# One plain float32 k-tile instead of two, six k-tiles of the first modulation summed on TensorE, idle matmuls and silu(c) at the head of a transformer block

## The chip, the cores and the metric

The kernel runs on one core of a Trainium2 chip. The metric is the device time of one execution in microseconds (us), lower is better; the median of several runs is compared.

## The reference, cut to what matters

One block of depth 1, with batch 1, T = 256 tokens, D = 2048 and float32 throughout. A vector c gives six rows of modulation (shift, scale and gate, for the mixer and for the feed-forward part), and x goes through a mixer and a feed-forward net:

```python
mod = jax.nn.silu(c) @ w_ada[l] + b_ada[l]                 # c: 1 x 2048, w_ada: 2048 x 12288
shift_m, scale_m, gate_m, shift_f, scale_f, gate_f = jnp.split(mod, 6, axis=-1)
h = modulate(rms_norm(x, pre_norm_mix[l]), shift_m, scale_m)   # h * (1 + scale) + shift
... = jnp.split(h @ w_in[l], split_at, axis=-1)             # w_in: 2048 x 5656
o = jnp.concatenate([nsa_mixer(...), moba_mixer(...)], axis=-1) @ w_o[l]
x = x + gate_m[:, None, :] * rms_norm(o, post_norm_mix[l])
h = modulate(rms_norm(x, pre_norm_ffn[l]), shift_f, scale_f)
f = jnp.square(jax.nn.relu(h @ w_up[l])) @ w_down[l]        # 2048 x 8192 and back
x = x + gate_f[:, None, :] * rms_norm(f, post_norm_ffn[l])
```

All weights together are some 300 MB, and each is read once.

## The kernel before, in words

**Products.** A k-tile is 128 of the 2048 columns of h. Nearly every product is made of three: activation and weight are each split into a high and a low part of type fp32r (`split`, L544 on ScalarE and L545 on VectorE for a weight, `split2`, L417 and L418 for an activation), and `products` (L549 to L551) multiplies high by high, high by low and low by high into one PSUM bank. Where k is under `M_PLAIN` (two k-tiles before), `weight_units` takes one plain float32 matmul instead (L497) and splits nothing; the trace shows such a matmul as two records.

**Modulation.** The rows shift and scale are needed as columns, one value a partition. `mod_units` makes them for 2 or 4 k-tiles at a time (`M_MODS`): `gemv_units` loads the matching columns of w_ada for all 2048 rows (L305), VectorE accumulates weight times silu(c) over 16 k-tiles of rows (L318 and L323), and TensorE adds the 128 partitions up. For the first group (tile `modm0`), the k-tiles in `M_DIRECT` (3, 7, 11) go to TensorE at once, as matmuls with a single column (`column_sums`, L359), and the accumulated rest follows with a column of ones. The bias enters by a matmul with the identity (L356). The other groups are transposed (L377) and reduced on VectorE (L379). Then ScalarE (L414) and, for the second k-tile, VectorE (L400) modulate `xnm`, the normalised and transposed x.

**The head.** `x_units` loads x in four pieces (L573), squares it on ScalarE (L579), scales it on VectorE (L584) and transposes it on TensorE (L283; L285 copies back). c is loaded first, b_ada and the two norms next (L205 to L208, ScalarE's queue); silu(c) is L189 to L214, `columns` L216 to L223.

**Order.** `Stream.run` walks a list of units. A unit has a load, a preparation (a split, or VectorE's accumulation) and a main part (products). At most `RAWBUFS` = 5 loaded tiles may be held: a tile is given back after its preparation, or for plain products after its main part. All loads go through SyncE's queue in list order. The list starts with x, the group `modm0`, then the blocks of w_in (kv, kw, qn, vm, km, qm, each 1024 columns wide, kw 536) for k = 0 and 1, with the eight loads and the end of the next group (`modm2`, k = 2 to 5) strewn between them by `spread` (L1000). Then come the blocks for k = 2 to 5 with the next group between them, and so on. The order of instructions on each engine is fixed when the program is built, from list order, priority (`high_priority`) and readiness; each engine then works in that order. `late_constants` (L244) loads the rope table and small weights amid this, and transposes `stageb` (L257).

**The end.** The last unit multiplies token-major. After a bank's last product, `down_done` squares it on ScalarE (L1229) and multiplies by the gate on VectorE (L1230); `finish` sums four squares (L269), makes the reciprocal root (L273, L274 on GpSimd) and writes x (L1238, L1241).

## Time and profile before

| | |
|---|---|
| three runs | 1189.11, 1190.44, 1192.91 us; median 1190.44 us |
| profiled execution | 1188.98 us, of which the span from first to last instruction is 1187.2 us |
| busy in the span | TensorE 1154.3 us, VectorE 901.4 us, ScalarE 592.8 us |
| DMA | 312.03 MB, mean 263 GB/s |

In the profile PE is TensorE (PEld its weight loads), DVE VectorE, ACT ScalarE, POOL GpSimd and SP SyncE; a q behind a name is the engine's queue, where DMAs are issued. Times in rows are us from the start of the span unless marked ns. TensorE is busy nearly throughout, so that what matters is where it waits, and what it does while it only seems busy.

### The profile page before, as it was taken

Reading aid. Unit: us, or ns where it says so; the run is one execution under the profiler, and the core shown is the slowest. Engines: PE = TensorE matmul, PEld = TensorE weight load, DVE = VectorE, ACT = ScalarE, POOL = GpSimd, SP = SyncE. Lnnn points to the kernel's source line nnn. Section 1 sums busy time; section 2 is a strip of 40 time slices with the busy share of each in tenths; the row PEclk is TensorE's granted clock in tenths of the full one; section 3 lists DMA queues with packets and bytes.
Section 4 is the critical chain, followed back from the end, with each engine's and each line's share of the span. In section 5 each row is a group of like instructions: output and inputs, shape, how many; then the busy total and the mean of one; then the engine's idle time right before and its main releaser. Section 6 shows DMA issues by size and latency. Waiting matters only on the chain.

```text
span 1187.2 us, 14413 instructions
## 1 busy us (share of the span) xinstructions
PE 1154.3 (97%) x5411; PEld 935.7 (79%) x5411; DVE 901.4 (76%) x1111; ACT 592.8 (50%) x908; POOL 13.5 (1%) x23
## 2 busy tenths in 40 slices
PE   5999999999999998999999999999999999999997
PEld 4468888877777786888888888888888888888885
DVE  5679999889999988777888986666576666665573
ACT  4353444438746658565343344767444434444441
POOL 1000000000000001000000000000000000000000
PEclk9999999999999999999999999999999999999999
DMA  9999998775867985988878976545677777775541
GB/s 333 370 394 326 334 362 295 238 281 176 316 213 258 327 337 200 367 285 305 290 249 300 315 248 204 172 152 208 238 244 270 255 258 264 259 268 187 203 142 71
DMA packets 92601, 312.03 MB, mean 263 GB/s; under 512 B 6306, under 2 KB 14962, under 8 KB 79602
## 3 DMA queue, kind: packets, MB, share of 16 engines
q1 hardware_dynamic: 92324, 311.04, 74.7%
q8 instruction: 42, 0.69, 0.2%
q14 instruction: 27, 0.22, 0.1%
q10 hardware_dynamic: 208, 0.07, 0.0%
HBM read 308.99 MB, written 2.10 MB: 262 GB/s over the span
## 4 chain that ended last, share of the span: by engine, by line
PE 88%; DVE 7%; ACT 1%; issue 1%; DMA 1%; POOL 0%; SPq 0%; DVEq 0%; POOLq 0%; ACTq 0%
PE dps L550 10%; PE dps L551 10%; PE dps L549 10%; PE up L551 9%; PE up L550 9%; PE up L549 9%; PE wo L550 2%; PE wo L549 1%; PE wo L551 1%; PE ft L1146 1%; PE in_qm L551 1%; PE in_qm L549 1%; PE in_qm L550 1%; PE in_km L549 1%; PE in_km L550 1%
## 5 line engine op out<-in xcount | busy, mean ns | idle before, releaser
L323 DVE SCALAR_TENSOR_TENSOR modm<-modm,csil,modm 128x1024 f32<-128x1024 f32 (+1 forms) x72 | 78.3, 1087 | 9.4 <-DMA modm<-in_w_ada_dram 8.0
L323 DVE SCALAR_TENSOR_TENSOR modf<-modf,csil,modf 128x1024 f32<-128x1024 f32 x60 | 76.8, 1280 | 5.6 <-DMA modf<-in_w_ada_dram 5.2
L1162 DVE TENSOR_TENSOR facc<-up,facc 128x512 f32<-128x512 f32 x96 | 61.5, 685 | 19.2 <-PE up L551 19.2
L323 DVE SCALAR_TENSOR_TENSOR gatef<-gatef,csil,gatef 128x1024 f32<-128x1024 f32 x32 | 40.6, 1280 | 1.7 <-DMA gatef<-in_w_ada_dram 1.7
L323 DVE SCALAR_TENSOR_TENSOR gatem<-gatem,csil,gatem 128x1024 f32<-128x1024 f32 x32 | 40.3, 1275 | 0.0
L1202 DVE TENSOR_TENSOR flo<-facc,fhi 128x512 fp32r<-128x512 f32 x32 | 21.8, 686 | 2.0 <-ACT fhi L1201 2.0
L1201 ACT CAST fhi<-facc 128x512 fp32r<-128x512 f32 x32 | 19.7, 624 | 5.3 <-PE up L550 1.9
L1164 ACT ACTIVATE facc<-facc 128x512 f32<-128x512 f32 x32 | 18.4, 623 | 2.8 <-DVE facc L1162 2.8
L1160 ACT COPY facc<-up 128x512 f32<-128x512 f32 x32 | 18.0, 586 | 1.7 <-PE up L551 1.0
L545 DVE TENSOR_TENSOR up_13lo<-up,up_13hi 128x1024 fp32r<-128x1024 f32 x8 | 9.8, 1226 | 11.5 <-ACT up_13hi L544 11.5
L545 DVE TENSOR_TENSOR up_14lo<-up,up_14hi 128x1024 fp32r<-128x1024 f32 x8 | 9.8, 1226 | 11.1 <-ACT up_14hi L544 11.1
L1151 ACT ACTIVATE facc<-ft 128x512 f32<-128x512 f32 x32 | 17.1, 586 | 0.4 <-PE ft L1146 0.2
L1146 PE MATMUL ft<-ident,facc 128*128 128x128 f32 x128 | 16.8, 273 | 0.0
L1146 PEld LDWEIGHTS ft<-ident,facc 128*128 128x128 f32 x128 | 14.7, 140 | 2.6 <-ACT facc L1151 0.4
L544 ACT CAST up_7hi<-up 128x1024 fp32r<-128x1024 f32 x8 | 8.4, 1056 | 14.2 <-PE up L551 14.2
L544 ACT CAST up_11hi<-up 128x1024 fp32r<-128x1024 f32 x8 | 8.4, 1056 | 14.2 <-PE up L551 14.2
L544 ACT CAST up_10hi<-up 128x1024 fp32r<-128x1024 f32 x8 | 8.4, 1056 | 13.3 <-PE up L551 13.3
L544 ACT CAST up_6hi<-up 128x1024 fp32r<-128x1024 f32 x8 | 8.4, 1056 | 13.3 <-PE up L551 13.3
L544 ACT CAST up_14hi<-up 128x1024 fp32r<-128x1024 f32 x8 | 8.4, 1049 | 12.6 <-PE up L551 12.6
L544 ACT CAST up_9hi<-up 128x1024 fp32r<-128x1024 f32 x8 | 8.4, 1056 | 12.1 <-DVE up_8lo L545 6.7
L544 ACT CAST up_8hi<-up 128x1024 fp32r<-128x1024 f32 x8 | 8.4, 1054 | 11.7 <-PE up L551 11.7
L544 ACT CAST up_5hi<-up 128x1024 fp32r<-128x1024 f32 x8 | 8.4, 1056 | 11.2 <-PE up L551 7.8
(2266 smaller groups left out, 3966.4 us busy)
## 6 DMA issues: line engine op xcount, KB each, us to landing
up<-in_w_up_dram SPq DMA_DIRECT2D x64, 1024.0 KB, 5.2
dn<-in_w_down_dram SPq DMA_DIRECT2D x64, 1024.0 KB, 5.0
modf<-in_w_ada_dram SPq DMA_DIRECT2D x64, 512.0 KB, 6.2
modm<-in_w_ada_dram SPq DMA_DIRECT2D x48, 512.0 KB, 7.1
gatem<-in_w_ada_dram SPq DMA_DIRECT2D x16, 1024.0 KB, 5.5
wo<-in_w_o_dram SPq DMA_DIRECT2D x16, 1024.0 KB, 6.3
gatef<-in_w_ada_dram SPq DMA_DIRECT2D x16, 1024.0 KB, 4.9
modm<-in_w_ada_dram SPq DMA_DIRECT2D x32, 256.0 KB, 6.0
```

The source lines that it names most:

```text
L323: nc.vector.scalar_tensor_tensor(part, w[:, j:j + step], csil[:, k:k + 1], part, ALU.mult, ALU.add)
L544: nc.scalar.copy(hi[:, 0:n], src)
L545: nc.vector.tensor_sub(lo[:, 0:n], src, hi[:, 0:n].bitcast(F32))
L549: nc.tensor.matmul(o, shi, whi, start=first, stop=False)
L550: nc.tensor.matmul(o, shi, wlo, start=False, stop=False)
L551: nc.tensor.matmul(o, slo, whi, start=False, stop=last)
L1146: nc.tensor.transpose(b[:, (2 * i + t) * P:(2 * i + t + 1) * P], f[:, t, (2 * j + i) * P:(2 * j + i + 1) * P], ident)
L1160: nc.scalar.copy(dst, b)
L1162: nc.vector.tensor_add(dst, b, dst)
L1164: nc.scalar.activation(dst, dst, AF.Relu)
L1201: nc.scalar.copy(hi, f)
L1202: nc.vector.tensor_sub(lo, f, hi.bitcast(F32))
```

## The change

- The second k-tile is split (`M_PLAIN` = 1): for k = 1 the six blocks of w_in and the activation are split as for later k-tiles. The tile that holds k = 0 and 1 is still given back after the main part.
- Six k-tiles of `modm0` (2, 5, 8, 11, 13, 14) go straight to TensorE instead of three, and the bias is added on VectorE at the end instead of by a matmul.
- Idle matmuls (`keep_warm`, float32 transposes of 128 x 128 into a bank that nobody reads): 56 ahead of everything but silu(c)'s own transpose, 24 behind the transposes of x's second half, 4 behind each of the six direct k-tiles.
- silu(c) is computed in a tile that the squares of x then reuse, so they wait for it; the loads of b_ada and of the norms come behind the first load of `modm0`, and `columns` is a unit behind the first two of `modm0`.
- The second half of x is scaled on ScalarE instead of VectorE.
- The loads and the end of `modm2` are put at written positions: the order of loads becomes kv, M, kw, M, qn, M, M, vm, M, km, M, M, qm, M (M is one load of `modm2`, 1 MB), with the end of `modm2` ahead of the second product unit of qm. It was kv, M, M, kw, M, M, qn, M, M, vm, M, M, km, qm.
- At the end, three of the four squares are summed beforehand (`final_rstd`), and the reciprocal root is issued ahead of the last multiplication by the gate.

```diff
-M_PLAIN = 2
-
-M_DIRECT = (3, 7, 11)
+M_PLAIN = 1
+
+M_DIRECT = (2, 5, 8, 11, 13, 14)
+
+WARM = (56, 24, 4)
...
-        sigmoid_parts(csil, pc[:, 0:KD])
-        nc.vector.reciprocal(csil, csil)
-        nc.vector.tensor_mul(csil, csil, pc[:, 0:KD])
+
+        sig = gp.tile([P, KD], F32, tag="ga", name="csig")
+        sigmoid_parts(sig, pc[:, 0:KD])
+        nc.vector.reciprocal(sig, sig)
+        nc.vector.tensor_mul(csil, sig, pc[:, 0:KD])
+    warm = mbank("warm")
+
+    def keep_warm(src, n):
+        for i in range(n):
+            nc.tensor.transpose(warm[:, (i % 4) * P:(i % 4 + 1) * P], src, ident)
+
+    keep_warm(ident, WARM[0])
...
         def column_sums(w, v, stop):
...
-            if "b" not in sums:
+            fresh = "b" not in sums
+            if fresh:
                 sums["b"] = bank(f"{name}t")
-                nc.tensor.matmul(sums["b"][:, 0:2 * nk].rearrange("p (s k) -> p s k", s=2), ident,
-                                 bias[:, :, ks], start=True, stop=False, skip_group_check=True)
...
         def direct(k, w):
             column_sums(w, csil[:, k:k + 1], False)
+            keep_warm(w[:, 0:P], WARM[2])
...
-                b = sums["b"]
-                nc.vector.tensor_mul(red[:, nk:], b[:, nk:2 * nk], gcol[:, ks])
-                nc.vector.tensor_copy(red[:, 0:nk], b[:, 0:nk])
+                nc.vector.tensor_add(red.rearrange("p (s k) -> p s k", s=2),
+                                     sums["b"][:, 0:2 * nk].rearrange("p (s k) -> p s k", s=2),
+                                     bias[:, :, ks])
+                nc.vector.tensor_mul(red[:, nk:], red[:, nk:], gcol[:, ks])
...
-                    if k % 2 and not (tag == "m" and k < M_PLAIN):
+                    if k % 2:
                         stat[k // 2] = (pair(f"{name}hi{k}", F32R), pair(f"{name}lo{k}", F32R))
-                        split2(xv, *stat[k // 2])
+                        i = M_PLAIN if early else 0
+                        split2(xv[:, i:, :], *(v[:, i:, :] for v in stat[k // 2]))
...
-                unsplit = ks[i0] < plain
+                unsplit = k0 + kk < plain
                 u = Unit(load if kk == 0 else None, None if unsplit else prep, main,
                          w=0 if unsplit or i0 + kk in spare else 1,
-                         free=None if kk == 0 else "main" if unsplit else "prep")
+                         free=None if kk == 0 else "main" if k0 < plain else "prep")
...
                 for v in st["x"]:
-                    nc.vector.tensor_scalar(v, v, r, None, ALU.mult)
+                    if t:
+                        nc.scalar.mul(v, v, r)
+                    else:
+                        nc.vector.tensor_scalar(v, v, r, None, ALU.mult)
...
             transposed(f"xt{t}", lambda k: st["x"][k // 8][:, (k % 8) * P:(k % 8 + 1) * P], xnm, t)
+            if t:
+                keep_warm(st["x"][1][:, 0:P], WARM[1])
...
     m0[0].load = load_first
-    stream.add(xu + m0)
+    stream.add(xu + m0[:2] + [Unit(None, columns)] + m0[2:])
     base = flat(in_units(n, 0, 2) for n in ("kv", "kw", "qn", "vm", "km")) + turn0[:2]
-    stream.add(spread(base, mods[1], 1, len(base) - 1))
+    for j, at in enumerate((2, 5, 8, 9, 12, 15, 16, 18, 19)):
+        base[at:at] = mods[1][j]
+    stream.add(base)
...
         nc.scalar.activation(junk, b, AF.Square, accum_out=fsq[t][:, n:n + 1])
+        if n >= 2:
+            with tc.high_priority():
+                final_rstd(n, t)
         nc.vector.tensor_mul(fg[n][:, t, :], b, gate_f["G"][:, n * 512:(n + 1) * 512])
+
+    def final_rstd(n, t):
+
+        s, r = frstd[t]
+        if n == 2:
+            nc.vector.tensor_reduce(s, fsq[t][:, 0:3], axis=AX.X, op=ALU.add)
+            nc.vector.tensor_scalar(s, s, 1.0 / D, EPS, ALU.mult, ALU.add)
+        else:
+            nc.vector.tensor_scalar(r, fsq[t][:, 3:4], 1.0 / D, s, ALU.mult, ALU.add)
+            nc.gpsimd.tensor_tensor(r, r, mhalf, ALU.pow)
```

## Rows read from the trace of the kernel before

**Rows 1.** The page, part 1: busy us of each engine.
```profile
PE 1154.3 (97%) x5411; PEld 935.7 (79%) x5411; DVE 901.4 (76%) x1111; ACT 592.8 (50%) x908; POOL 13.5 (1%) x23
```
**Rows 2.** Waits of PE, whole span: waited for, us in total, times, longest.
```profile
PE in_vm L497 <- DMA in_vm<-in_w_in_dram: 1.4, 1, 1.4
```
**Rows 3.** Timeline of PE: start, us, line, operation, tiles, shapes, records [idle before].
```profile
16.38 5.01 PE L283 MATMUL xt<-ident,x 128*128 128x128 f32 x21
21.18 1.71 PE L359 MATMUL modm0t<-csil,modm 128*128 128x1 f32 x8
...
27.84 9.44 PE L497 MATMUL in_kv<-in_kv,xnm 128*128 128x512 f32 x16 [1.01 <-ACT xnm L414]
...
40.73 7.03 PE L497 MATMUL in_qn<-in_qn,xnm 128*128 128x512 f32 x16
```
**Rows 4.** Timeline of PEld, the first products: start, us.
```profile
32.27 0.31 PEld L497 LDWEIGHTS in_kv<-in_kv,xnm 128*128 128x128 f32 x1 [0.52 <-issue]
32.83 0.19 PEld L497 LDWEIGHTS in_kv<-in_kv,xnm 128*128 128x128 f32 x1 [0.24 <-issue]
```
**Rows 5.** Timeline of PE, the first split products, k = 2.
```profile
71.36 0.39 PE L551 MATMUL in_qm<-in_qm_2hi,modm2lo 128*128 128x512 f32 x1
71.59 0.40 PE L549 MATMUL in_qm<-in_qm_2hi,modm2hi 128*128 128x512 f32 x1
```
**Rows 6.** Windows: stretch, length, busy of each engine (instructions), granted clock, DMA share, GB/s.
```profile
20.00:60.00 40.00, 37.63 (x112) 21.82 (x112) 26.80 (x30) 12.63 (x28) 0.00 (x0) 1.00 1.02 375
...
35.00:45.00 10.00, 10.00 (x32) 5.87 (x31) 6.32 (x5) 3.62 (x8) 0.00 (x0) 1.00 0.96 324
60.00:92.00 32.00, 32.00 (x117) 21.52 (x116) 23.05 (x21) 17.52 (x25) 0.00 (x0) 1.00 1.04 395
92.00:205.00 113.00, 112.28 (x545) 93.67 (x544) 109.95 (x132) 48.73 (x58) 0.00 (x0) 1.00 0.94 330
```
**Rows 7.** Line 305, its last load of the first group: issue, us to landing.
```profile
L305 SPq DMA_DIRECT2D modm<-in_w_ada_dram x1: 368/368/368, 16.5 to 16.5; - x1
...
DMA to landing us min/median/max: 6.0/6.0/6.0
```
**Rows 8.** Timeline of DVE, from the second group's end to in_vm.
```profile
50.44 5.34 DVE L323 SCALAR_TENSOR_TENSOR modm<-modm,csil,modm 128x1024 f32<-128x1024 f32 x4 [2.63 <-DMA modm<-in_w_ada_dram]
...
60.60 0.69 DVE L418 TENSOR_TENSOR modm2lo<-xnm,modm2hi 128x512 fp32r<-128x512 f32 x1 [2.22 <-ACT modm2hi L417]
...
66.05 1.23 DVE L545 TENSOR_TENSOR in_qm_2lo<-in_qm,in_qm_2hi 128x1024 fp32r<-128x1024 f32 x1 [1.62 <-ACT in_qm_2hi L544]
...
91.66 1.37 DVE L633 TENSOR_TENSOR km<-in_km,km 128x512 f32<-128x512 f32 x2 [2.51 <-PE in_km L551]
92.95 1.22 DVE L545 TENSOR_TENSOR in_vm_2lo<-in_vm,in_vm_2hi 128x1024 fp32r<-128x1024 f32 x1
```
**Rows 9.** Timeline of ACT, the split of in_vm's weights.
```profile
88.50 1.06 ACT L544 CAST in_vm_2hi<-in_vm 128x1024 fp32r<-128x1024 f32 x1 [1.80 <-DMA in_vm<-in_w_in_dram]
```
**Rows 10.** Timeline of PE, a product that waits for VectorE's split.
```profile
124.81 0.50 PE L550 MATMUL in_kv<-in_kv_4lo,modm2hi 128*128 128x512 f32 x1 [0.19 <-DVE in_kv_4lo L545]
```
**Rows 11.** Late constants: PE's transpose; the last small load (L249), issue and landing.
```profile
85.23 0.27 PE L257 MATMUL pconst<-ident,stageb 64*128 64x64 f32 x1
...
L249 SPq DMA_DIRECT2D stageb<-in_cmp_v_pos_dram x1: 318/318/318, 75.5 to 75.5; - x1
...
DMA to landing us min/median/max: 8.0/8.0/8.0
```
**Rows 12.** Timeline of DVE at the end.
```profile
1179.20 0.16 DVE L269 TENSOR_REDUCE fr<-fsq 128x1 f32<-128x4 f32 x1 [2.03 <-ACT junk L1229]
1179.28 0.68 DVE L1230 TENSOR_TENSOR fg<-dps,gatef 128x512 f32<-128x512 f32 x1
1179.88 0.14 DVE L273 TENSOR_SCALAR fr<-fr 128x1 f32<-128x1 f32 x1
1180.77 2.74 DVE L1238 SCALAR_TENSOR_TENSOR x<-fg,fr,x 128x512 f32<-128x512 f32 x4 [0.75 <-POOL fr L274]
```

## What the change should do to the time

> **What bounds the kernel now.** I read the page's busy times first, then the waits of TensorE, its timeline up to 72 us, the loads and VectorE in the same stretch, and the end. TensorE is busy for 1154.3 of 1187.2 us [rows 1], so the question is where its time before the first product, its slow products and its few waits go. Four things are to be seen.
>
> First, the head. TensorE's first real product starts at 27.84 us [rows 3]. Until then it transposes x and adds up the first modulation. The last weight tile for that is issued at 16.5 and lands 6.0 later, at 22.5 us [rows 7].
>
> Second, TensorE's clock. The granted clock reads 1.00 in every window [rows 6], but durations say that the early part ran at the lower of the two levels, 1.2 GHz: a weight load takes 0.31 us at 32.27 and 0.19 at 32.83 [rows 4], and in_kv's 16 records take 9.44 us where in_qn's take 7.03 [rows 3]. So the clock rose to 2.4 GHz 4.7 us after the products had begun. The transposes of x, 21 in a row for 5.01 us, ran ahead of it at 1.2 GHz and did not raise it.
>
> Third, the loads. From 20 to 92 us the DMA share is 1.02 to 1.04 [rows 6], and the consumers stand right behind the landings: in_vm's products waited 1.4 us for their weights [rows 2], and the later tile of in_vm was split the moment it landed [rows 9]. This stretch is paced by memory at about 395 GB/s, 2.65 us a megabyte tile, and TensorE just keeps up. A faster TensorE alone is not enough here.
>
> Fourth, VectorE. From 92 to 205 us it is busy for 109.95 of 113 us, TensorE for 112.28 [rows 6], and a product waits for VectorE's half of a split at 124.81 [rows 10]. What is gained ahead of 92 us outlives this stretch only if VectorE also starts it earlier. It does start late for TensorE's sake: at 91.66 it had idled 2.51 us for the sums of in_km [rows 8].
>
> **The change part by part.** The sum is made against the profiled execution, 1188.98 us (span 1187.2 and 1.8 around it). It is the fastest of the times shown; the median of the three runs is 1.46 higher, and I add the gain to that median.
>
> *One plain k-tile instead of two.* A plain 512-wide record starts every 7.03 / 16 = 0.43 us, after the overlap of the last, and a plain product has two, 0.86. The split one has three records 0.23 apart [rows 5], 0.68. Five wide blocks have four such products for k = 1: 20 x 0.18 = 3.5 us less, and kw, a half as wide, 0.3 less: 3.8 us. It costs ScalarE six casts of up to 1.06 [rows 9] and VectorE six subtractions of up to 1.22 [rows 8], some 6 and 7 us. VectorE was busy for 26.80 of the 40 us from 20 to 60 [rows 6], so 13 us of idle time hide it; without that cover it would cost up to 7.
>
> *The clock.* If the products start at 2.4 GHz, in_kv loses 9.44 - 7.03 = 2.4 us. With the wait of in_vm (1.4) gone, TensorE could reach its first split product of k = 2, at 71.1 us before, 3.8 + 2.4 + 1.4 = 7.6 us earlier, even with an unchanged first product.
>
> *The head.* Six direct k-tiles leave VectorE ten instead of thirteen, silu(c) ready early takes it out of the queue behind x, and the second half of x goes to ScalarE, which only squares and copies there. VectorE can then follow the landings, and the first product can come after 22.5, one accumulation, the closing sums and the modulation: 25.5 to 26 at the earliest. TensorE pays for three more sets of sums (1.71 each at 1.2 GHz [rows 3]) and 56 + 24 + 24 = 104 idle transposes. At x's spacing, 5.01 / 21 = 0.24 us, these take 25 us at 1.2 GHz and about 12 at 2.4. At the higher clock everything fits: about 3.4 us for c, 16 for 136 transposes, 6 for sums, so 26 to 28, and I take the first product as unmoved. The cover is good: of the 7.6 us only some 4 can be used (next), so a start up to 31 us costs nothing.
>
> *The order of loads.* In the new order the last load of the second group comes behind km and qm, two megabyte tiles or 5.3 us later. Memory itself gains a little: from 35 to 45 us its share fell to 0.96 because loads waited for given-back tiles [rows 6], 0.08 of 10 us, and in the new order a tile comes free sooner. I take 0.7 us (bounds 0, and 1.8 if the whole drop from 395 to 324 GB/s comes back). So that last load lands 4.6 us later than before. There its accumulation ended at 55.8, and the low half of the activation it feeds at 61.3 [rows 8]; now 60.4 and 65.9. The first split weights of k = 2 were ready at 67.3 [rows 8] and used at 71.1; now ready at 66.6. TensorE can be 4.5 us early here, not 7.6.
>
> *What memory lets through.* The tightest point is the later tile of in_vm: cast from 88.50 [rows 9], so its low half could be ready at 88.50 + 1.06 + 1.22 = 90.8 if VectorE came straight to it. It was ready at 94.17 [rows 8], held by the sums of in_km. With TensorE 4 us early these sums are done by then: 3.4 from there plus 0.7 from memory is 4.1 us. VectorE enters its full stretch as much earlier, and nothing in it changes. I take 3.9 (bounds 2.4, below, and 5.2 with memory's 1.8).
>
> *The end.* The gate multiplication (0.68, at 1179.28) ran between the sum of squares and the step that GpSimd waits for (1179.88); the next one starts at 1180.77 [rows 12]. With the short step ahead of it and the sum down to one operation, GpSimd starts some 0.68 earlier and works beside the multiplication: 0.7 us less. Cost: four tiny operations more on VectorE, ahead of the end, beside products.
>
> *Edits with no price.* The bias on VectorE instead of a matmul, `columns` later and the loads of b_ada later all lie ahead of 22.5 us, beside loads. The squares of x wait for silu(c), which needs only c.
>
> Sum: 3.9 + 0.7 = 4.6 us, so 1184.4 against the profiled execution and 1190.44 - 4.6 = **1185.8** as a median, 0.4% faster.
>
> *A rule against it.* The rows show transposes at 1.2 GHz throughout, 5.01 us in a row and no rise [rows 3], but with single-column sums on both sides, so they don't show what 56 in a row do. The Trainium skill ("TensorE: Matmul & The Clock Gate", Part 4: PE-mode transpose) says that the full clock does not engage for transposes, since they don't count as busy in the same way. By that rule the second rival below would come true; the trace agrees as far as it goes.
>
> **The rivals.** *A fixed arrival stops the gain early (within 0.3%).* TensorE transposes the late constants at 85.23; their last load was issued at 75.5 and landed at 83.5 [rows 11], memory-paced, so now at 82.8. If the new order on TensorE keeps this transpose where it stood among the products of in_km, the products behind it wait, and TensorE can be only 85.2 - 82.8 = 2.4 us early. That is handed to VectorE at 91.66 and stays: 2.4 + 0.7 = 3.1, so 1187.3. Any loss of 1.5 us or more of VectorE's head start ends here too. For it: the code of that unit is not touched. Against it: the order on an engine is made anew, and the transpose stood 1.7 us behind its landing.
>
> *The idle matmuls stay at 1.2 GHz (slower).* Then the head is TensorE's: from 3.4 us, 104 x 0.24 = 25 us of idle transposes, the 14 us of real work that stood between 12.6 and 26.8, and 5 for three more sets of sums put the first product at about 47.5 instead of 27.8, 19.7 later. Of that the split gives back 3.8, in_vm's wait 1.4 and the end 0.7; the clock rises only under the products, as before. 1190.4 + 13.8 = 1204; with idle transposes at 0.21 apart, 1201. I put 1203 (1198 to 1206). It decides as soon as the first product falls behind 27.8 + 5.9 = 33.7. For it: 5.01 us of transposes without a rise. Against: that run was cut by sums of one column, and 56 in a row are more than twice as long.
>
> *The change brings more than its loads allow* has no mechanism that I see: beyond memory's 1.8 us it needs bytes that have not landed.
>
> **How the numbers follow.** Forecast 0.56, its own range 1184 to 1186.9. Early stop 0.26 (1186.9 to 1190). Idle matmuls at 1.2 GHz 0.18 (1198 to 1206): one rule and a cut run speak for it, no row shows it for an unbroken run. I leave this last one outside: 1183.5 to 1190.0 then holds 0.8, where 1183.5 takes in memory's upper bound (5.2 + 0.7 = 5.9, or 1184.5) and a run's spread. Faster by over 0.3% (3.6 us, about what a measurement of this kernel can tell from no change) is the forecast, 0.56; within 0.3% 0.26; slower 0.18.
>
> **What would show it.** Right: weight loads of in_kv at 0.19 us from the first one on; in_qn's and later first-tile blocks at 0.68 us for each k = 1 product; a first product at 26 to 31 us; TensorE waiting for DMA at in_vm and again at in_qm (1 to 2 us each); the first k = 2 product near 66.5; the sums of in_km on VectorE near 87.7, with no idle time ahead of them; the last multiplications (now after the reciprocal root) 0.7 sooner behind the last square. Wrong: L257's transpose preceded by a wait for a DMA; VectorE idle by more than 3 us between 92 and 205; or transposes 0.21 to 0.24 us apart up to a first product beyond 34 us. If the first product comes early but in_vm's later tile is not split sooner, the step from memory to VectorE is what failed.

## The result: slower by 0.9%, where faster was forecast

| | kernel before | changed kernel |
|---|---|---|
| time, median of 6 runs | 1190.2 us | 1201.88 us (1199.57 to 1204.73) |
| ratio to before | 1 | 1.0093, 95% interval 1.0075 to 1.0112 |
| profiled execution, its span | 1188.98, 1187.2 us | 1201.41, 1199.6 us |
| first product of TensorE | 27.84 us | 34.22 us |
| bytes loaded, 0 to 100 us | 367 GB/s | 334 GB/s |

The forecast was 1185.8 us (1183.5 to 1190.0). The page's busy times of the changed kernel beside [rows 1]: TensorE gained 14.7 us of busy time, 150 instructions and 12.4 us of span. Each trace shows one execution, and executions of one kernel differ: those of the kernel before took 1188.7 us (median of 8) where their mean granted clock was 0.998, as in its trace, and 1193.2 us (median of 9) where it was 0.991, and the traced executions of e2, e6, e9 and e13 below were the longest of their kernels (1199.53, 1202.48, 1206.37 and 1195.51 us).

```profile
PE 1169.0 (97%) x5561; PEld 957.5 (80%) x5561; DVE 903.2 (75%) x1115; ACT 600.8 (50%) x917; POOL 12.6 (1%) x23
```

TensorE's timeline of the changed kernel up to the first product (start, us, line, records; beside [rows 3]) shows the new head. L220 are the idle matmuls, L373 the direct sums, L296 x's transposes, L514 plain products:

```profile
3.32 9.09 PE L220 MATMUL warm<-ident 128*128 128x128 f32 x56
12.24 0.95 PE L373 MATMUL modm0t<-csil,modm 128*128 128x1 f32 x8
...
15.74 1.81 PE L296 MATMUL xt<-ident,x 128*128 128x128 f32 x8
17.34 1.71 PE L373 MATMUL modm0t<-csil,modm 128*128 128x1 f32 x8
...
27.11 2.46 PE L220 MATMUL warm<-ident,x 128*128 128x128 f32 x21
29.40 0.95 PE L373 MATMUL modm0t<-csil,modm 128*128 128x1 f32 x8
...
34.22 6.42 PE L514 MATMUL in_kv<-in_kv,xnm 128*128 128x512 f32 x8 [1.20 <-ACT xnm L431]
```

VectorE had the last tile of the first group in hand by 23.52 us (its timeline, below), so 34.22 is TensorE's own queue: idle matmuls, transposes and sums up to 33.

```profile
22.77 0.75 DVE L336 SCALAR_TENSOR_TENSOR modm<-modm,csil,modm 128x512 f32<-128x512 f32 x1 [2.47 <-DMA modm<-in_w_ada_dram]
29.01 1.22 DVE L562 TENSOR_TENSOR in_kv_1lo<-in_kv,in_kv_1hi 128x1024 fp32r<-128x1024 f32 x1 [5.49 <-ACT in_kv_1hi L561]
```

The waits of SyncE's DMA queue from 20 to 60 us (line, waited for, us, times, longest) show where that reaches the loads. A loaded tile goes back only when TensorE has used it, so loads stood 12.5 us behind idle matmuls:

```profile
SPq L493 <- PE warm L220: 7.8, 1, 7.8
SPq L318 <- PE warm L220: 4.7, 1, 4.7
SPq L318 <- PE in_kv L514: 4.6, 1, 4.6
```

Not all of this is the idle matmuls' doing. In e1 below, which has none, in_qn's load (7.8 us here) waits for a direct sum instead, 5.2 us, and goes out at 30.15 instead of 33.05; its loads from 28 to 60 us are no faster, 280 GB/s where the changed kernel has 291.

The windows of the changed kernel (columns as in [rows 6]) give the loads' pace in bytes: 310 GB/s from 20 to 60 us where [rows 6] have 375, and 364 after it instead of 395. TensorE loses 6 of the 32 us from 60 to 92.

```profile
20.00:60.00 40.00, 38.80 (x176) 28.77 (x175) 18.22 (x20) 16.93 (x35) 0.00 (x0) 0.84 0.88 310
35.00:45.00 10.00, 10.00 (x29) 5.94 (x27) 3.55 (x5) 3.29 (x5) 0.00 (x0) 0.76 0.83 294
60.00:92.00 32.00, 26.12 (x94) 18.14 (x92) 28.30 (x28) 14.35 (x21) 0.00 (x0) 0.89 0.98 364
92.00:205.00 113.00, 112.28 (x544) 93.46 (x543) 105.54 (x125) 49.25 (x61) 0.00 (x0) 1.00 0.94 330
```

Those 6 us are one place. TensorE is 6.1 us late against the kernel before at in_kw's first product, but only 1.0 at in_qm's (65.03, before: 64.04): shorter products for k = 1, no wait at in_vm and the sum not yet done have made up the head's delay. Then it loses 9.4 us. In its timeline the second group's sum, modm2t, stands at 70.70 (before: 56.06), and the first product that needs it waits 5.16 us. Then the products are 0.43 us apart up to 84 us, where [rows 5] have 0.23:

```profile
70.70 1.09 PE L392 MATMUL modm2t<-ident,modm 128*128 128x128 f32 x8 [0.71 <-DVE modm L336]
...
78.36 1.65 PE L566 MATMUL in_qm<-in_qm_2hi,modm2hi 128*128 128x512 f32 x3 [5.16 <-ACT in_qm_2hi L561]
...
81.42 0.63 PE L568 MATMUL in_qm<-in_qm_2hi,modm2lo 128*128 128x512 f32 x1
81.85 0.63 PE L567 MATMUL in_qm<-in_qm_2lo,modm2hi 128*128 128x512 f32 x1
```

The sum could not have gone sooner here. It waits 0.71 us for VectorE, which ends the accumulation behind it at 70.65 (its timeline; before: 55.78, [rows 8]):

```profile
68.05 2.60 DVE L336 SCALAR_TENSOR_TENSOR modm<-modm,csil,modm 128x1024 f32<-128x1024 f32 x2
```

### The profile page after: what moved, and what is told of

It is laid out like the page before. It is cut to its first block, busy times and chain, and to the rows that moved or that the text cites. A ratio compares the mean times of both kernels' runs of the same rounds, so it can differ in the third digit from the quotient of the medians.

```text
span 1199.6 us, 14731 instructions
## 1 busy us (share of the span) xinstructions
PE 1169.0 (97%) x5561; PEld 957.5 (80%) x5561; DVE 903.2 (75%) x1115; ACT 600.8 (50%) x917; POOL 12.6 (1%) x23
## 4 chain that ended last, share of the span: by engine, by line
PE 83%; DVE 8%; DMA 3%; issue 3%; ACT 2%; POOL 0%; ACTq 0%; SPq 0%; DVEq 0%; POOLq 0%
PE dps L568 9%; PE dps L567 9%; PE dps L566 9%; PE up L566 8%; PE up L568 8%; PE up L567 8%; DMA modf<-in_w_ada_dram 2%; PE wo L567 2%; PE wo L566 1%; PE wo L568 1%; PE ft L1170 1%; PE in_qm L566 1%; PE in_qm L567 1%; PE in_qm L568 1%; PE in_kv L567 1%
## 5 line engine op out<-in xcount | busy, mean ns | idle before, releaser
L336 DVE SCALAR_TENSOR_TENSOR modm<-modm,csil,modm 128x1024 f32<-128x1024 f32 (+1 forms) x69 | 75.6, 1096 | 3.7 <-DMA modm<-in_w_ada_dram 2.7
L1225 ACT CAST fhi<-facc 128x512 fp32r<-128x512 f32 x32 | 19.7, 624 | 5.3 <-PE up L567 1.9
L1170 PEld LDWEIGHTS ft<-ident,facc 128*128 128x128 f32 x128 | 14.7, 140 | 2.6 <-ACT facc L1175 0.5
```

The source lines that it names most:

```text
L336: nc.vector.scalar_tensor_tensor(part, w[:, j:j + step], csil[:, k:k + 1], part, ALU.mult, ALU.add)
L1170: nc.tensor.transpose(b[:, (2 * i + t) * P:(2 * i + t + 1) * P], f[:, t, (2 * j + i) * P:(2 * j + i + 1) * P], ident)
L1225: nc.scalar.copy(hi, f)
```

## The experiments

The change has separable parts; most were taken out of the changed kernel, or put alone into the kernel before. The explanations carry names:

- Theory 1: the idle matmuls, queued ahead of real work, make the loss.
- Rival A: the six direct k-tiles and the split of k = 1 do. Theory 2: the direct k-tiles do, and the order of loads by itself.
- Rival B: the order of loads does. Theory 3: the order costs nothing by itself; the loads are late because the first product is.
- Theories 4 to 6 came later and stand with their runs.

The kernel before was run beside each group and took 1189.3 to 1190.2 us there (medians), so a time is compared by its ratio. "Late at in_vm_13" is how much later than in the kernel before (313.01 us) TensorE reaches the first product with in_vm's k-tile 13, read from its timeline: it sums up what happens before that, most of it in the first 100 us, and nothing of what comes later.

| kernel | time, us | ratio to before, 95% interval | first product | GB/s 0 to 100 | late at in_vm_13 |
|---|---|---|---|---|---|
| changed | 1201.88 | 1.0075 to 1.0112 | 34.22 | 334 | 10.0 |
| e1 no idle matmuls | 1198.17 | 1.0057 to 1.0092 | 32.97 | 338 | 8.7 |
| e2 the 56 alone | 1195.32 | 1.0022 to 1.0050 | 32.78 | 334 | 9.6 |
| e3 old order of loads | 1195.53 | 1.0032 to 1.0059 | 36.76 | 338 | 6.6 |
| e4 idle matmuls in before | 1195.41 | 1.0032 to 1.0073 | 35.51 | 347 | 5.3 |
| e5 no idle, old order | 1195.63 | 1.0032 to 1.0066 | 33.63 | 339 | 5.9 |
| e6 no idle, three direct | 1199.82 | 1.0057 to 1.0105 | 30.47 | 351 | 5.2 |
| e7 both, the rest stays | 1191.28 | 0.9996 to 1.0021 | 31.20 | 361 | 0.8 |
| e8 as e7, two plain k-tiles | 1192.47 | 1.0014 to 1.0038 | 30.01 | 357 | 3.1 |
| e9 sum ahead again | 1199.73 | 1.0055 to 1.0112 | 36.24 | 336 | 9.1 |
| e10 new order in before | 1195.54 | 1.0031 to 1.0066 | 27.26 | 351 | 4.5 |
| e11 as e7, columns ahead | 1191.37 | 0.9989 to 1.0020 | 28.16 | 373 | -2.0 |
| e12 as e11, list of e9 | 1193.15 | 1.0010 to 1.0043 | 28.38 | 366 | 1.2 |
| e13 two terms in before | 1192.95 | 1.0011 to 1.0036 | 27.49 | 360 | 1.3 |
| e14 six direct in before | 1193.56 | 1.0018 to 1.0045 | 27.25 | 364 | 1.1 |
| e15 as e1, columns ahead | 1196.32 | 1.0033 to 1.0076 | 32.48 | 343 | 6.9 |
| e16 as e5, columns ahead | 1194.50 | 1.0012 to 1.0046 | 32.27 | 348 | 3.6 |

### e1 to e4: are the idle matmuls the cause?

```diff
e1:  -WARM = (56, 24, 4)   and the bank "warm" taken away
     +WARM = (0, 0, 0)
e2:  +WARM = (56, 0, 0)
e3:  -    for j, at in enumerate((2, 5, 8, 9, 12, 15, 16, 18, 19)): base[at:at] = mods[1][j]
     -    stream.add(base)
     +    stream.add(spread(base, mods[1], 1, len(base) - 1))
e4 (in before):  the changed kernel's keep_warm and its three calls, WARM = (56, 24, 4)
```

> The changed kernel without any of its idle matmuls (the 56 ahead of the work, the 24 after x's second half, the 4 after each weight tile's direct k-tiles) and without their bank; they are no part of the output. Theory 1: they stand in TensorE's in-order queue and, because a loaded tile is held until TensorE has used its direct k-tiles, they also hold back loads. Then the first product starts at 25 to 28 us instead of 34.22, the last load of the second group lands some 6 to 12 us earlier than 76.98, the wait of 5.16 us at in_qm_2hi goes or falls under 1 us, and the time falls from 1201.9 to 1185 to 1189. Rival A (the six direct k-tiles and the split of k=1 cost the time by themselves): the first product stays past 32 us and the time at 1197 or more. Rival B (the order of the loads in the second group): the first product is earlier but the wait of some 5 us at in_qm_2hi stays, and the time is 1191 to 1196.

> The changed kernel with the 56 idle matmuls ahead of the work alone; the 24 after x's second half and the 4 after each tile's direct k-tiles are left out, and are no part of the output. Theory 1 puts the cost in both places: x's first half still cannot be transposed before the 56 have ended (12.41 us in the changed kernel), but the later queue is shorter by 24 and 24 products, about 1.1 us per four at 1.2 GHz and 2.46 us for the block of 21 rows: first product at 27 to 31 us, time 1187 to 1194. If the 56 were what costs (they fill TensorE while the first loads come), the first product stays at 32 us or later and the time at 1197 or more. If the clock is still at full speed from the 56 when the products begin, none would show the granted clock at half at 30 us.

> The changed kernel with the second group's modulation loads spread evenly among the others, as in the kernel before; all else as changed. Rival B: the order by hand is what lets in_qm's second part come 12 us late, so its wait of 5.16 us goes, and the clock does not fall at 77 us: 1192 to 1196. Theory 1: the loads are late because they stood still from 24.61 to 33.05 us, so the order moves the wait but does not take it away: 1198 to 1204, first product still at 33 to 35 us.

> The kernel before with the changed kernel's idle matmuls alone (56 ahead of the work, 24 after x's second half, 4 after each of its three direct k-tiles' tiles); all else as before. Theory 1: they delay the first product from 27.84 to 31 us or later, and hold back loads as in the changed kernel, but with three direct k-tiles instead of six: 1193 to 1202 against 1190.2. Rival A: with three direct k-tiles the sums end early and TensorE has room for idle matmuls: 1189 to 1191, within measurement of no change. If they do what they stand for, the clock is at full speed from before the first product and the time falls by the 2.4 us that the start of the products lost to it: about 1188.

Theory 1 fell as the whole cause. Without any idle matmul (e1) the first product still starts at 32.97, the time is in Rival A's range, and the wait of 5.16 us stands where it did. Only some 1.3 us of lateness go (more in e15, below, where a side effect of the removal is taken out). In VectorE's timeline of e1 the sums are what it waits for, 6.95 us where the kernel before has 2.04:

```profile
31.86 0.16 DVE L402 TENSOR_TENSOR modm0red<-modm0t,cola 128x4 f32<-128x4 f32 x1 [6.95 <-PE modm0t L372]
```

In a kernel without the other parts (e4) the idle matmuls do cost 5 us. There they do what they stand for, in_kv's 16 records take 7.03 us instead of 9.44, but the first product comes 7.7 us later for it. e3 was faster than theory 1 allows and within what Rival B, the order of loads, said: its first product is the latest of all, at 36.76, and still 3.4 us of lateness go. e2 missed too: first product at 32.78 instead of 27 to 31, and half the clock from 14.9 to 38.8 us, so nothing of the 56 was left when the products began. By its median it is faster than e1, though its trace is later at in_vm_13; the traced execution took 4.2 us more than that median, so the two don't contradict each other.

### e5 to e8: direct k-tiles, order, and what is left

```diff
e5:  e1 and e3 together
e6:  e1 and  -M_DIRECT = (2, 5, 8, 11, 13, 14)   +M_DIRECT = (3, 7, 11)
e7:  e1, e3 and e6's M_DIRECT
e8:  e7 and  -M_PLAIN = 1   +M_PLAIN = 2   (k = 0 and 1 unsplit)
```

> The changed kernel without its idle matmuls and with the second group's loads spread as in the kernel before; the six direct k-tiles stay. Theory 2 (each direct k-tile more costs TensorE eight sums of about 0.2 us, 1.6 us in all, in a queue that was already the last to end ahead of the first product; the order of the loads costs the rest): first product at 32 to 33 us as without the idle matmuls, but no wait of 5 us at in_qm_2hi: 1190 to 1194. Theory 3 (the order costs nothing by itself; the loads are late because the first product is): the wait at in_qm_2hi stays and the time is 1196 to 1199. If the sums were free, the first product would stand at 28 us and the time at 1185 to 1188.

> The changed kernel without its idle matmuls and with the three direct k-tiles (3, 7, 11) of the kernel before; the new order of the second group's loads stays. Theory 2: first product at 27 to 28.5 us, and the wait at in_qm_2hi stays (2 to 5 us, with the fall of the clock behind it), since the weight tiles that stand ahead of the modulation tiles hold the buffers: 1190 to 1195. Theory 3: the loads come some 5 us earlier with the first product, the wait goes or is under 1 us: 1185 to 1188.

> The changed kernel without its idle matmuls, with three direct k-tiles and with the loads spread as before: of the change there remain the split of k=1, silu(c) ahead of x, the bias added on VectorE and the mean squares' sums ahead of the end. Theories 2 and 3 alike: first product at 27 to 28.5 us, no wait of over 1 us but the one at in_vm, in_kv to in_qm's first parts 3.8 us shorter as far as the loads let them, the end 0.7 us shorter: 1185 to 1188.5. Rival: between 28 and 71 us the loads set the pace and not TensorE, so that what the split saves turns into waits for in_vm, in_km and in_qm: 1188.5 to 1190.5 (the end alone).

> As the kernel before it (no idle matmuls, three direct k-tiles, the loads spread as before), but with both first k-tiles as plain float32 products again: silu(c) ahead of x, the bias on VectorE and the sums ahead of the end remain. If the split of k=1 is worth its 3.8 us of TensorE, this is 2 to 3.8 us slower than that kernel, at 1188.5 to 1190. If the loads set the pace there, the two are within 0.7 us of each other.

None of the four times lies in a range written down for it: e5's falls between two of them, the others are longer than all. In the signs theory 2 holds so far: order and direct k-tiles each cost by themselves. e6 and e7 differ in the order of loads alone, by 8.5 us of time and 4.4 of lateness, and e6 has the wait of 5.16 us with its loads at 351 GB/s (changed kernel: 334) and its first product 3.8 us sooner. So theory 3 fell as the cause of the wait. e5 and e7 differ in the direct k-tiles: 4.4 us of time, 5.1 of lateness. e7 against e8 gives the split of k=1: 2.3 us of lateness, 1.2 of time (the intervals overlap), where 3.8 had been counted.

What nobody had expected is e8: the parts that I had given no price make the kernel slower than before by 0.14 to 0.38%. Its first product starts at 30.01. TensorE's timeline of e8 shows where it begins: a direct sum waits for its weights until 12.64, and the transpose of the bias columns (L231), moved behind it, waits with it.

```profile
12.64 1.84 PE L372 MATMUL modm0t<-csil,modm 128*128 128x1 f32 x8 [9.07 <-DMA modm<-in_w_ada_dram]
14.34 0.45 PE L231 MATMUL pconst<-ident,stagea 128*128 128x128 f32 x1
```

VectorE's copy of that transpose was queued ahead of x's reduction, so VectorE idled 9.74 us with x's first squares long done, and x was scaled from 16.12 us (before: 10.91):

```profile
14.83 0.29 DVE L232 COPY cola<-pconst 128x128 f32<-128x128 f32 x1 [9.74 <-PE pconst L231]
15.04 0.14 DVE L281 TENSOR_REDUCE xr<-xss 128x1 f32<-128x2 f32 x1
...
16.12 1.42 DVE L603 TENSOR_SCALAR x<-x,xr 128x1024 f32<-128x1024 f32 x2 [0.66 <-POOL xr L286]
```

In the changed kernel itself VectorE's queue has that copy behind x, and x is scaled from 9.95 us. This price is one of e1 and e5 to e8 only, where taking the idle matmuls away had changed that order.

### e9 to e12: which part of the order costs

Theory 4: not the loads' places but the sum's make the price. The list puts the last two modulation units behind in_qm's first part, so modm2t stands behind all products that could cover the way from it by VectorE and ScalarE to modm2hi.

```diff
e9:   -enumerate((2, 5, 8, 9, 12, 15, 16, 18, 19))
      +enumerate((2, 5, 8, 9, 12, 13, 15, 16, 17))
e10 (in before):  the changed kernel's list in place of spread(...), nothing else
e11 = e7 and  +    columns()                (ahead of the stream, its loads ahead of x)
              -    stream.add(xu + m0[:2] + [Unit(None, columns)] + m0[2:])
              +    stream.add(xu + m0)
e12 = e11 with e9's list
```

> The changed kernel with the last four modulation units of the second group put earlier in the list (places 13, 15, 16, 17 instead of 15, 16, 18, 19, so that the group's sum stands ahead of in_km's second unit as in the kernel before); all else as changed, idle matmuls and six direct k-tiles included. Theory 4 (the list moved the group's sum on TensorE, modm2t, behind all of in_km's and in_qm's first products, so nothing is left in its queue to cover the way by VectorE and ScalarE to modm2hi; the wait of 5.16 us and the fall of the clock behind it are the price): modm2t stands some 12 us earlier, the wait goes, the clock stays up: 1193 to 1197. Theory 3 (the loads are late with the first product): the wait stays in some form, 1199 to 1203.

> The kernel before with the changed kernel's list of places for the second group's modulation units, and nothing else of the change. Theory 4: the first product stays at 28 us, modm2t moves from 56 to 70 us, a wait of about 5.2 us opens ahead of in_qm_2hi, the clock falls for some 7 us behind it (another 2 to 2.5 us), and the wait of 1.36 us for in_vm's load goes: 1194 to 1198 against 1190. Theory 3: no wait of over 2 us at in_qm_2hi, 1188 to 1191.

> The kernel e7 (the split of k=1, silu(c) ahead of x, the bias on VectorE, the sums ahead of the end; three direct k-tiles, the old order of loads, no idle matmuls) with the loads and the transpose of the bias and gain columns put back to where the kernel before has them, ahead of x and of the first group. Theory 5 (in e7 that transpose stands behind the first direct k-tile in TensorE's queue and waits with it for its weights, to 15.53 us, and VectorE's copy of its result stands ahead of x's reduction in VectorE's queue, so x is scaled from 17.31 instead of 10.91 us and the first product starts at 31.20 instead of 27.84): x is scaled by 13 us, the first product starts at 26.5 to 28.5 us: 1186 to 1189. Rival: the loads set the pace from there to 71 us, and the 3.4 us turn into waits for in_kw, in_qn and in_vm: 1189.5 to 1192.

> The kernel e11 with the list of places of e9 (the weight tiles ahead, the second group's sum still ahead of in_km's second unit) instead of the even spread. Theory 4 with 5: as e11, and the wait for in_vm's load (1.3 us) goes as it did with the new list in e6, without the wait at in_qm_2hi: 1185 to 1188. If the list costs in another way (the modulation loads come later than the sum needs them), a wait of 1 to 4 us stands at modm2t, and the time is 1189 to 1193.

e10 shows theory 4 in the kernel before with nothing else moved. The first product is not late (27.26), and TensorE's timeline has the sum at 66.48, only 1.88 us of products behind it, then the wait:

```profile
61.33 5.31 PE L497 MATMUL in_qm<-in_qm,xnm 128*128 128x512 f32 x12
66.48 1.04 PE L377 MATMUL modm2t<-ident,modm 128*128 128x128 f32 x8
67.35 1.88 PE L497 MATMUL in_qm<-in_qm,xnm 128*128 128x512 f32 x4
74.13 1.65 PE L549 MATMUL in_qm<-in_qm_2hi,modm2hi 128*128 128x512 f32 x3 [4.90 <-ACT in_qm_2hi L544]
```

TensorE stood 2.7 us ahead of the kernel before at in_qm's first product and 4.9 behind it at in_qm's k-tile 4. Time 1195.5, as expected. VectorE had ended the accumulation at 63.15 and sat idle 3.96 us for the sum, so by my estimate some 3.3 of the 4.9 us are the sum's place, and the rest is the later load.

e9 missed, and its time is in theory 3's range. The wait at in_qm_2hi went, as theory 4 says, but 0.9 us of lateness is all that went with it. The sum came at 69.25 instead of some 12 us earlier, since VectorE ended the accumulation only at 69.20. Two other waits stand in its place, in TensorE's waits of e9 from 20 to 130 us:

```profile
PE in_km L566 <- ACT in_km_4hi L561: 2.2, 1, 2.2
PE modm2t L392 <- DVE modm L336: 2.0, 1, 2.0
```

With idle matmuls and six direct k-tiles still in the kernel its loads run at 336 GB/s over the first 100 us, and its first product is 2.0 us later than the changed kernel's. So in the changed kernel the accumulation is late as well as the sum, and either hides the other. e12, with the early head, has the same two waits (2.3 and 1.8 us) and is 3.2 us later than e11 at in_vm_13; its time lies just above the second of its two forecasts. So a list with the weight tiles ahead costs even where the sum is put right.

e11 confirms theory 5 on the head, not on the time, which is in the rival's range. x is scaled from 13.45 us, the first product starts at 28.16, the loads run at 373 GB/s, and TensorE is 2.0 us early at in_vm_13, the only kernel that is early at all. The time shows nothing of it: 0.9989 to 1.0020. In the traced execution 2.8 us were lost between 357 and 457 us; the window of TensorE there has a clock of 0.96, where the same window of before reads 1.00:

```profile
370.00:450.00 80.00, 77.72 (x359) 63.81 (x360) 70.39 (x96) 49.01 (x103) 0.55 (x1) 0.96 0.82 291
```

### e13 and e14: the forecast's own terms, alone

```diff
e13 (in before):  M_PLAIN = 1 with k = 1 split, and final_rstd ahead of the end
e14 (in before):  -M_DIRECT = (3, 7, 11)   +M_DIRECT = (2, 5, 8, 11, 13, 14)
```

> The kernel before with two parts of the change alone: k=1 split (k=0 alone as plain float32 products), and the mean squares' sums ahead of the end. As the prediction counted: 3.8 us less of TensorE in in_kv to in_qm and 0.7 us less at the end, 1185 to 1187. Theory 6 (in_kv to in_km's split parts run at the pace of the loads, 391 GB/s from 60 to 100 us in the kernel before, and what the split saves comes back as waits for loads unless the loads too start earlier): the first product at 27.5 to 28.5 us, 0 to 2 us of the 3.8 left past 100 us, waits ahead of in_vm, modm2t or in_km_4 in their place: 1187 to 1189.5.

> The kernel before with the changed kernel's six direct k-tiles (2, 5, 8, 11, 13, 14) instead of its three, and nothing else of the change. Theory 2: 24 more sums on TensorE at 1.2 GHz, 1.6 us for each eight, so the first product starts at 31 to 33 us instead of 27.84 while VectorE is done with its part by 22 to 24 us; the loaded tiles are held as long, the loads from 28 to 60 us fall from 371 GB/s to 280 to 330, and TensorE is 4 to 6 us late past 100 us: 1193 to 1196. Rival (TensorE has room for them ahead of the first product): first product by 28.5 us and 1189 to 1191.

e13 is the run that decides on the forecast: its two gains, with every other part left out, make the kernel slower by 0.11 to 0.36%. Theory 6, that the loads take the gain back, missed too: the time is above its 1187 to 1189.5, and the first wait is at in_qn, which it did not name. SyncE's timeline of e13 shows how. Its four modulation loads ahead of in_qn's take 9.85 us, where the kernel before needs 4.88, and in_qn's load goes out at 34.53 instead of 32.27:

```profile
24.59 9.85 SPq L305 DMA_DIRECT2D modm<-in_w_ada_dram  x4
34.53 0.42 SPq L479 DMA_DIRECT2D in_qn<-in_w_in_dram  x1
```

The third of them stood still up to 32.98, and the waits of SyncE's queue from 20 to 60 us say for what: for in_kv's loaded tile, first until its subtraction on VectorE had ended, then until its plain products had (the first two lines, e13). In the kernel before the load that waits for in_kv's products (the third line) comes behind in_qn's and not ahead of it. Why the tiles are dealt out otherwise no run tells.

```profile
SPq L305 <- DVE in_kv_1lo L548: 4.5, 1, 4.5
SPq L305 <- PE in_kv L500: 3.0, 1, 3.0
SPq L305 <- PE in_kv L497: 4.7, 1, 4.7
```

In VectorE's timeline of e13 the subtraction, behind a short wait for ScalarE, stands ahead of the second group's accumulation, which starts at 29.85 (before: 27.54):

```profile
28.71 1.23 DVE L548 TENSOR_TENSOR in_kv_1lo<-in_kv,in_kv_1hi 128x1024 fp32r<-128x1024 f32 x1 [0.52 <-ACT in_kv_1hi L547]
29.85 0.75 DVE L318 TENSOR_SCALAR modm<-modm,csil 128x1024 f32<-128x1024 f32 x1
```

TensorE, 1.6 us early at in_kw, waits 2.9 us for in_qn; the clock was at 0.52 behind that, from 41 to 48 us. The sum modm2t then waits 2.0 us for VectorE, whose last accumulations stood behind in_vm's subtraction, and that had waited 3.6 us for ScalarE. At in_km TensorE is 3.5 us late, at in_vm_13 1.3, where some 4 us early had been counted. The rest of what this execution lost came behind 350 us, beside falls of the clock (0.83 from 370 to 380 and from 420 to 430 us).

e14 has theory 2's time and the rival's head: alone, six direct k-tiles don't delay the first product (27.25). Its loads do run at 358 GB/s from 28 to 60 us instead of 371, and TensorE waits 1.5 us for in_qn beside the 1.6 for in_vm that the kernel before has nearly as long [rows 2]; of its 3.4 us, 1.1 are there at in_vm_13. But in this execution the clock was up for a while ahead of the products: TensorE's timeline has eight direct sums in 1.71 us at 12.87, and 32 in 3.63 at 21.41, half the time for each.

```profile
12.87 1.71 PE L359 MATMUL modm0t<-csil,modm 128*128 128x1 f32 x8
...
21.41 3.63 PE L359 MATMUL modm0t<-csil,modm 128*128 128x1 f32 x32
```

### e15 and e16: idle matmuls and direct k-tiles without the side effect

```diff
e15 = e1 and  columns() ahead, as in e11
e16 = e5 and  columns() ahead, as in e11
```

> e1 (the changed kernel without its idle matmuls) with the bias and gain columns' loads and transpose ahead of x, as in e11. In e1 the removal alone had put x's scaling from 9.95 to 15.63 us, a side effect that hid part of what the idle matmuls cost. If they cost the head as they do in the kernel before (7.7 us in e4), x is scaled by 13.5 us, the first product starts at 28 to 30.5 us, the wait of 5 us at in_qm_2hi stays (the new order), TensorE is 4.5 to 6 us late at in_vm_13 and the time is 1194 to 1197: the idle matmuls are then worth 5 to 7 of the changed kernel's 11.7 us. If six direct k-tiles hold the head by themselves, the first product stays past 32 us and the time at 1197 to 1199.

> e15 with the old, even spread of the second group's loads: of the change there remain the split of k=1, six direct k-tiles, silu(c) ahead of x, the bias on VectorE and the sums ahead of the end. Against e11 it differs in the three direct k-tiles more. As e14 has them: no later first product (28 to 29.5 us), 1 to 3 us later at in_vm_13 than e11's -2.0, 1190.5 to 1194. If e5's five us belong to them: first product past 31 us, 4 us or more late at in_vm_13, 1194.5 to 1197.

x is scaled from 13.61 and 13.16 us, and still the first product comes at 32.48 and 32.27, against 28.16 in e11, which has three direct k-tiles. For e15 a first product at 28 to 30.5 had been expected: its time is in the first of the two ranges, its first product in the second. TensorE's timeline of e15 is full from 16 us on, and each direct k-tile takes its 1.71 us at the lower clock:

```profile
22.84 2.31 PE L297 MATMUL xt<-ident,x 128*128 128x128 f32 x9
24.94 1.71 PE L374 MATMUL modm0t<-csil,modm 128*128 128x1 f32 x8
26.51 1.52 PE L297 MATMUL xt<-ident,x 128*128 128x128 f32 x6
27.82 1.71 PE L374 MATMUL modm0t<-csil,modm 128*128 128x1 f32 x8
```

So theory 2 stands where the clock is down: three k-tiles more make the head 4.1 us later (e16 against e11), TensorE 5.7 us later at in_vm_13 and the time 3.1 us longer (the intervals overlap a little). The idle matmuls are worth 5.6 us of time and 3.1 of lateness in the changed kernel (against e15). With the old order (e3 against e16) they are worth as much lateness, 3.0, but 1.0 us of time, so their price in time is not settled; in e4 it was 5.5.

One step at a time, the 10.0 us of lateness come apart: 3.1 go with the idle matmuls (changed kernel to e15, where the columns move ahead too), 3.2 with the new order (e15 to e16), 5.7 with three direct k-tiles (e16 to e11), and what is left is 2.0 us early. The order's part is 2.8 to 4.5 us in all five pairs that differ in it alone; the time of these pairs differs by 1.8 to 8.5 us.

## Why the prediction was wrong, step by step

*One plain k-tile instead of two, -3.8 us.* The size on TensorE was right: in_kv to in_qm take 6.2 us a block (46.52 for in_qn's first record, 52.69 for in_vm's) instead of some 7. The step that failed is its cover: "13 us of idle time hide it". I compared busy times in a window. What counted in e13 is who waits for the added operation: a load waited 4.5 us for in_kv's subtraction and 3.0 for its plain products, and accumulations stood behind in_vm's subtraction. e13: no gain, 2.8 us of loss by the medians, of which 1.3 are seen at in_vm_13. The split is not a loss everywhere: between e8 and e7 it brings 2.3 us of lateness.

*The head, taken as unmoved, cover up to 31 us.* It went to 34.22. I let all 104 idle transposes run at the higher clock; the row has 2.46 us for a block of 21 but 9.09 for the first 56 and a clock of 0.50 from 15.8 to 26.1 us. Of the 6.4 us the idle matmuls are 1.7 (changed kernel against e15) and the three direct k-tiles more 4.1 (e16 against e11), which I had priced at 1.71 each and then let fit in at the higher clock. The step itself failed too: "a start up to 31 us costs nothing" forgot that tiles are held until TensorE has used them. e7 and e11 differ in the head alone: a first product at 31.20 instead of 28.16 makes the loads from 28 to 60 us 350 instead of 380 GB/s and TensorE 2.8 us later at in_vm_13.

*The order of loads, 4.6 us later, k = 2 products at 66.5.* They came at 78.36. This is where the forecast is farthest off, and where the lateness shows: 9.4 us arise between in_qm's first product and its k-tile 4. (The order alone is worth 2.8 to 4.5 us by in_vm_13, since ahead of in_qm it gains: in e10 TensorE is 2.7 us early there.) I moved the load and VectorE's accumulation behind it, to an end at 60.4, and left TensorE's modm2t where it was among the products. e10, with an early head, has the accumulation's end at 63.15 and the sum 3.3 us behind it, since the list had put it behind in_qm's first products: a wait of 4.9 us with the clock's fall behind it. In the changed kernel the accumulation itself ended at 70.65, behind the late loads.

*What memory lets through, 3.9 us.* It took the DMA share as full. From 28 to 60 us it fell from 371 to 291 GB/s. VectorE enters its full stretch late and not early (105.54 us busy from 92 to 205 us instead of 109.95).

*The end, -0.7 us.* Right. In VectorE's last rows (beside [rows 12]) the reduction or its substitute to the last multiplication takes 0.88 us instead of 1.57:

```profile
1192.21 0.21 DVE L1268 TENSOR_SCALAR fr<-fsq,fr 128x1 f32<-128x1 f32 x1 [1.91 <-ACT junk L1253]
1192.34 0.68 DVE L1257 TENSOR_TENSOR fg<-dps,gatef 128x512 f32<-128x512 f32 x1
1193.09 2.74 DVE L1276 SCALAR_TENSOR_TENSOR x<-fg,fr,x 128x512 f32<-128x512 f32 x4
```

*Edits with no price.* Wrong in e8: a transpose moved behind a direct sum that waits for a load, and behind it, on another engine, x. That they "all lie ahead of 22.5 us, beside loads" looked at time and not at the queues.

*The rivals.* The early stop at the late constants did not come up: they landed at 91.88 and were transposed at 95.26. "The idle matmuls stay at 1.2 GHz" gave 1203 (1198 to 1206), which holds the time, but by luck and not by its mechanism: it wanted the first product at 47.5, and the clock did rise. Its 19.7 us of head were 6.4; the rest is the order and the loads. Of the signs of being wrong two came: VectorE idle for 7.5 us between 92 and 205 (before: 3.1), and a first product beyond 34 us, though not with transposes at the lower clock up to it. The rule from the Trainium skill that spoke for it ("TensorE: Matmul & The Clock Gate", Part 4: PE-mode transpose: the full clock does not engage for transposes) is not borne out here for float32 transposes: nothing but transposes ran before 9.0 us, and from there they are twice as fast (below).

*What stays open.* The parts alone cost 0.5, 0.5, 0.3 and 0.2% (e10, e4, e14, e13), 1.6% in sum, and 12.2 us of lateness; together they cost 0.9% and 10.0 us. So they overlap, but which covers which is not shown for each pair. Of the changed kernel's 12.4 us of span, 10.0 are there at in_vm_13. The other 3.0 on TensorE (the end gives 0.7 back) come later: 1.0 by 397 us, behind two waits of 1.0 and 1.1 us at 379 and 381 that the kernel before has as well, there without a fall of the clock; 2.0 at 575, where a product waits 1.7 us for VectorE. What decides on either no run tells. The 2 us that e11's traced execution gains early are lost there too; whether this is why none of its ten times shows them is not shown.

## What to carry to other kernels

Idle time in a window hides nothing by itself: ask which load waits for the buffer that the added operation reads, and what stands behind it in its engine's queue. When loads set the pace, every delay of a buffer's last reader is a delay of memory, and an idle or early instruction in an in-order queue is not free even if its engine has nothing else to do. When a load is moved in a list, follow everything that the list moves with it, down to the small sum on the engine that sets the end, and count the products left behind that sum against the way through the other engines.

## What the hardware did that was not expected

TensorE's clock rose under transposes alone. In the changed kernel, 28 records took the 5.80 us up to 9.00 and 34 the next 3.40, 0.21 and 0.10 us each (the granted clock reads 1.00 for both; the step is in the durations). Single-column sums, idle transposes and waits followed, and the granted clock was 0.50 from 15.8 (windows of TensorE):

```profile
3.20:9.00 5.80, 5.80 (x28) 5.76 (x29) 1.19 (x7) 3.67 (x8) 0.00 (x0) 1.00 0.94 322
9.00:12.40 3.40, 3.40 (x34) 3.40 (x32) 2.37 (x8) 2.30 (x4) 0.63 (x2) 1.00 1.06 368
...
15.80:26.10 10.30, 10.30 (x52) 10.30 (x51) 4.77 (x9) 3.42 (x11) 0.00 (x0) 0.50 1.07 374
```

In e14, too, 15 transposes of x in a row (3.73 us) stood ahead of the sums that ran at the higher clock, while [rows 3] have 21 with none behind them faster, and e13 has the same 21 (5.01 us) with sums of 1.15 and 0.95 us behind them instead of 1.71. What decides is open. A wait of 4.9 to 5.2 us ahead of in_qm_2hi was followed by products at the lower clock in the changed kernel and in e1, e2, e6, e10 and e15. In the changed kernel this made 2.6 us more: TensorE was 7.9 us late at in_qm_2hi and 10.4 at in_qm_4hi. In the others it made 1.3 (e10) to 2.5 us (e1).
